# Channel-major tokens, a one-block start, and another entry to the second layer, in a two-layer hybrid backbone

## Chip, cores and metric

The kernel runs on one core of one Trainium2 chip. The metric is the device time of one execution in microseconds (us); less is better.

## The reference, cut to what matters

Two layers over 256 latent tokens `x` and 256 context tokens `ctx`, each 2048 wide, batch 1. Everything is float32.

```python
# layer 0                                   # layer 1
shift, scale, gate = adaln(c, ada_w[i], ada_b[i])      # silu(c) @ w + b, split in three
h = modulate(rms_norm(x, norm_g[i]), shift, scale)     # h*(1+scale)+shift
hc = the same for ctx with c_ctx                       # layer 0 alone
p = h @ w_in ; pc = hc @ w_in[:, COL_K:]    # p = h @ sc_in, four parts
neighbourhood attention (16 heads) on q, k, v, k_ctx, v_ctx
bidirectional SSD scan (32 heads)           # short gated convolution
out = concat(ya, yb) @ w_out                # out = (silu(g) * y) @ sc_out
x = x + gate * out                          # x = x + gate * out
```

The modulation vector of layer 0 needs `ada_w[0]`, 2048 x 6144 floats; of it, the scale columns (from 2048) and the shift columns (from 0) are needed before any projection can start, the gate only at the layer's end.

## The kernel before

One generator program records all instructions. Small tasks (generators) wait for a condition and an engine, and a planner (`Plan`) keeps a due time for each engine and tile: `pump` emits a task's next step when the planner's times say it is ready, `force` emits whatever is needed to go on. So the order of the instructions on each engine's queue is fixed when the program is built, out of costs written into `Plan`; among them `RATE`, the bytes per ns that it counts for a load, and 1500 ns that it adds to a transfer issued from another queue than SP's.

Large matmuls keep float32 accuracy by three products: an operand is split in a high part (a cast on ScalarE, `wH`, `hH`) and a low part (the difference, on VectorE, `wL`, `hL`), and high*high, low*high and high*low are summed. Weights come as pieces of 512 KB, 128 partitions x 1024 floats, into a pool of five `raw` buffers plus four borrowed ones (`PT`, `xtm`, `yi`), and are split into `NW` = 3 buffers `wH`/`wL`. All these loads stand in one queue, `loads`, and are issued by SP in that order (`issue`).

First stage of layer 0, over eight pairs `j` of 128-channel blocks `kb` = 2j, 2j+1:
- `x_load` brings tokens token-major, four tiles of 128 x 512 for each row tile of 128 tokens. `x_norm` squares each with a row sum on ScalarE or VectorE, takes the reciprocal root (`rstd`: VectorE, then a power on GpSimd) and scales the tile. `x_pair` turns it on TensorE (64 turns in all) into channel-major `xnT`. The context (`x_load(2)`, `x_load(3)`) is loaded behind the weights of pair 0.
- `ada_gen` multiplies the conditioning vectors (padded, `cpad`) by the modulation weights: for each pair, scale and shift, four pieces each of 512 rows x 256 columns. The sums go out of PSUM by ScalarE (L689), are turned, reduced and added on VectorE (L697 to L703) into `A0`, `S0`. Then `h = xnT*A0 + S0` is made once on ScalarE (high part, L719) and once on VectorE (L721), and subtracted (L725).
- The loop over `j` multiplies K, V (four row tiles, each into one bank, drained by `part_gen` into partial sums, L749 and L751), Q (two row tiles, accumulated over all pairs in two banks) and B (two banks). All matmuls are recorded at L188, turns at L192.

Behind it come the gate, dt, SSD and attention groups, all beside the large projections; then the output projection, columns 0 to 1023 first, then 1024 to 1535, then 1536 to 2047. `gemv_gen` multiplies the remaining modulation columns on VectorE (L776) in the background.

Entry to layer 1: `res_gen` forms `x1 = x + gate*out` for the last columns (L1506, L1509) and its squares (L1511); `turn_gen` turns `x1` to channel-major and scales it by `A1` into `late` (L1534); `norm_gen` waits for all four column groups, computes the norm factor, spreads it over the partitions through a diagonal and a matmul with ones (L1540 to L1544), and makes the sixteen blocks of `h1` (L1561, L1563, L1553).

Of the kernel before, what the change touches and what calls it, by code (L numbers as in the profile page):

```python
# [23 lines left out]
for _name, _w in (("c", 16), ("cc", 16), ("g0", 16), ("ab0", 48), ("g1", 16), ("ab1", 48), ("cw", 160), ("cb", 32),  # L24
                  ("sg", 16), ("qg", 1), ("kg", 1), ("scw", 48), ("dtb", 1), ("alog", 1), ("dcol", 16)):
    _off[_name] = (_n, _n + _w)
    _n += _w
NSMALL, NFIRST = _n, 96
# [3 lines left out]
for _name, _w in (("ident", 128), ("sel", 2), ("mhalf", 32), ("strip", 640), ("mask", 64)):  # L32
    _coff[_name] = (_n, _n + _w)
    _n += _w
NCONST, CFIRST = _n, 162


class Plan:
# [3 lines left out]
    RATE = 270.0  # L42
# [55 lines left out]
    def add(self, b):  # L98
# [10 lines left out]
        if op == "DMACopy":  # L109
# [4 lines left out]
            if e == "SP":  # L114
                self.dma = max(self.dma, s + 1000) + n / self.RATE
                done = free = self.dma + 1000
            else:
                done = free = max(self.dma, s + 1000) + n / self.RATE + 1500
# [23 lines left out]
def kernel(ctx: ExitStack, tc, x, cx, ada_w, ada_b, w_in, w_out, sc_in, sc_out, rpb, small, const,  # L142
# [96 lines left out]
    def may(task, hor, isurg):  # L239
# [5 lines left out]
        if nb and len(free_b) < nb + (0 if isurg else reserve[0]):  # L245
            return False
        now, t = plan.t["PE"], plan.t["ACT" if eng == "AQ" else eng]
# [17 lines left out]
    halfsplit = []  # L265
# [70 lines left out]
    E(DMA.dma_start(sm[:, :NFIRST], small[:, :NFIRST]))  # L336
    cs_ = st([128, NCONST], "const")
    E(DMA.dma_start(cs_[:, :CFIRST], const[:, :CFIRST]))
# [15 lines left out]
    def issue():  # L354

        while (loads or later) and (free_r or (loads and callable(loads[0]))):
# [12 lines left out]
            E(DMA.dma_start(v, w[r0:r0 + nb * 128, c0:c0 + n].rearrange("(b p) c -> p b c", p=128)))  # L369
            RAW[key] = (raw, v)  # L370

    nw = [0]
    room = [2]

    def weight(w, r0, nb, c0, n):
        loads.append(("w", nw[0], w, r0, nb, c0, n, room[0]))
        nw[0] += 1

    def split():
# [3 lines left out]
        if n == 64:  # L383

            W = WH[k % NW].rearrange("p (b c) -> p b c", b=nb)
# [9 lines left out]
        E(S.copy(H, v))  # L395
        E(V.tensor_tensor(out=Lo, in0=v, in1=H.bitcast(F32), op=ALU.subtract))  # L396
        HL[k] = (H, Lo)
        pos["split"] += 1
        give_raw(raw)
        issue()  # L400

    def split_half(b):

        raw, v = RAW[0]
        H, Lo = (w[0].rearrange("p (b c) -> p b c", b=2) for w in (WH, WL))
        E(S.copy(H[:, b], v[:, b]))

        def rest():
            E(V.tensor_tensor(out=Lo[:, b], in0=v[:, b], in1=H[:, b].bitcast(F32), op=ALU.subtract))  # L409
            if b:  # L410
                RAW.pop(0)
                HL[0] = (H, Lo)
                pos["split"] += 1
                give_raw(raw)
                issue()

        halfsplit.append(rest)

    def splits_try():
        if hold[0]:  # L420
            return
        while pos["split"] < pos["use"] + NW and pos["split"] in RAW:
            if plan.ready([RAW[pos["split"]][1]]) > max(plan.t["PE"], plan.t["ACT"]) + 300:
                return
            split()

    def use(ahead=0):
        k = pos["use"] + ahead
        while pos["split"] <= k:
# [4 lines left out]
            split()  # L434
        splits_try()
# [7 lines left out]
    def q_ada(j, *parts):  # L443
        for part, base in ((0, 2048), (1, 0)):
            if parts and part not in parts:
                continue
            for q in range(4):
                loads.append(("a", ("ada", j, part, q), ada_w[0], q * 512, 4, base + j * 256, 256, 2))
# [36 lines left out]
    q_ada(0)  # L485
    w_seg(0, CK, CV, CQ)
    loads.append(lambda: x_load(2))
    loads.append(lambda: x_load(3))
# [43 lines left out]
    ssq = st([128, 16], "ssq")  # L532

    def x_load(t):
        src = x if t < 2 else cx
        r0 = (t % 2) * 128
        for q in range(4):
            xt = st([128, 512], f"hH{4 * t + q}", name=f"xs{4 * t + q}")
            E(DMA.dma_start(xt, src[r0:r0 + 128, q * 512:(q + 1) * 512]))
            XS[4 * t + q] = xt  # L540

    x_load(0)
    x_load(1)
    issue()
    bs1 = st([128, 16], "bs1")
    E(V.tensor_scalar(out=bs1, in0=P_("ab0")[:, 16:32], scalar1=1.0, scalar2=None, op0=ALU.add))
    xnT = [st([128, 512], ("Bl", "Cl")[kb] if kb < 2 else f"hL{kb}", name=f"xm{kb}") for kb in range(KB)]
    rx = st([128, 4], "rx")

    def x_norm(t):  # L550
        yield when(lambda: 4 * t + 3 in XS and (t < 2 or ("h", 0, 0) in got))
        for q in range(4):
            xt = XS[4 * t + q]
            yield W_("ACT" if q % 2 == 0 else "DVE", xt)
            jk = tmp()
            if q % 2 == 0:
                E(S.activation(jk, xt, AF.Square, accum_out=ssq[:, 4 * t + q:4 * t + q + 1]))
            else:
                E(V.tensor_tensor_reduce(out=jk, in0=xt, in1=xt, scale=1.0, scalar=0.0, op0=ALU.mult, op1=ALU.add,
                                         accum_out=ssq[:, 4 * t + q:4 * t + q + 1]))  # L560
            give(free_t, jk)
        yield W_("DVE", ssq[:, 4 * t:4 * t + 4])
        E(V.tensor_reduce(out=rx[:, t:t + 1], in_=ssq[:, 4 * t:4 * t + 4], axis=AX.X, op=ALU.add))
        rstd(rx[:, t:t + 1], rx[:, t:t + 1], D, EPS, 1)
        for q in range(4):
            xt = XS[4 * t + q]
            yield W_("DVE" if q % 2 else "ACT", rx[:, t:t + 1])
            if q % 2 == 0:
                E(S.mul(xt, xt, rx[:, t:t + 1]))
            else:  # L570
                E(V.tensor_scalar(out=xt, in0=xt, scalar1=rx[:, t:t + 1], scalar2=None, op0=ALU.mult))

    def x_pair(k2, ts):

        yield W_("PE", *[XS[4 * t + k2 // 2] for t in ts], nb=1)
        ps = bank()
        n = 128 * len(ts)
        for k in range(2):
            kb = 2 * k2 + k
            for i, t in enumerate(ts):  # L580
                turn(ps[:, k * n + i * 128:k * n + (i + 1) * 128], XS[4 * t + kb // 4][:, (kb % 4) * 128:(kb % 4) * 128 + 128])
        yield W_("ACT", ps)
        o = slice(ts[0] * 128, ts[0] * 128 + n)
        E(S.copy(xnT[2 * k2][:, o], ps[:, 0:n]))
        E(V.tensor_copy(xnT[2 * k2 + 1][:, o], ps[:, n:2 * n]))
        give(free_b, ps)
        got.update(("xm", t, k2) for t in ts)

    def x_gen(c):

        ts = (2 * c, 2 * c + 1)
        for t in ts:
            yield from x_norm(t)
            if c:
                yield from x_pair(0, (t,))
        for k2 in range(c, KB // 2):
            yield from x_pair(k2, ts)
# [68 lines left out]

    def ada_gen():
        bc = lambda ap: ap.unsqueeze(2).to_broadcast([128, 2, 2])
        for j in range(8):
            k2 = slice(2 * j, 2 * j + 2)  # L670
            for part, dst in ((0, A0), (1, S0)):
                ps = None
                for q in range(4):
                    key = ("ada", j, part, q)
                    w_ = 2 if j == 0 else 4
                    if q % w_ == 0:
                        ks = [("ada", j, part, q + i) for i in range(w_)]
                        yield when(lambda: all(k in RAW for k in ks))
                        yield W_("PE", *[RAW[k][1] for k in ks], nb=0 if ps is not None else 1)
                    if ps is None:  # L680
                        ps = bank()
                    raw, v = RAW.pop(key)
                    for g in range(4):
                        mm(ps[32 * g:32 * g + 32, :256], cpad[:, 4 * q + g, :], v[:, g, :], q == 0, q == 3)
                    give_raw(raw)
                    issue()
                yield W_("ACT", ps)
                Rt = half()
                E(S.copy(Rt, ps[:, :256]))  # L689

                yield W_("PE", Rt)
                for b in range(2):
                    turn(ps[:, 256 + b * 128:384 + b * 128], Rt[:, b * 128:(b + 1) * 128])
                give(free_h, Rt)
                yield W_("DVE", ps)
                p2 = dst[:, k2, :]
                E(V.tensor_reduce(out=p2, in_=ps[:, 256:].rearrange("p (b g c) -> p b c g", b=2, c=32)[:, :, 0:2, :],  # L697
                                  axis=AX.X, op=ALU.add))
                if part == 0:
                    E(V.tensor_tensor(out=dst[:, k2, :], in0=p2, in1=bc(bs1[:, k2]), op=ALU.add))  # L700
                    E(V.tensor_tensor(out=dst[:, k2, :], in0=dst[:, k2, :], in1=bc(g0[:, k2]), op=ALU.mult))
                else:
                    E(V.tensor_tensor(out=dst[:, k2, :], in0=p2, in1=bc(P_("ab0")[:, k2]), op=ALU.add))  # L703
                give(free_b, ps)

# [832 lines left out]
    def norm_gen():  # L1538
# [19 lines left out]
        for kb in range(KB):  # L1558
# [5 lines left out]
            if kb:  # L1564
                low(kb - 1)
# [192 lines left out]
```

## Time and profile before

| | us |
|---|---|
| median of three runs | 1822.08 (1821.28 to 1822.44) |
| the profiled execution | 1820.64 |
| its span | 1818.9 |
| TensorE busy in the span | 1785.2 (98%) |
| VectorE busy | 1259.2 (69%) |
| ScalarE busy | 777.4 (43%) |
| moved by DMA | 376.9 MB, 207 GB/s in the mean |

A share of busy time is a mean over stages with different limits; what a change in one stage is worth is read from the gaps of the busiest engine there. L12 in a row is line 12 of the kernel before; PE is TensorE, PEld its weight loads, DVE VectorE, ACT ScalarE, POOL GpSimd, SP the load queue's engine.

### The profile page before, as it was taken

To read this page: it belongs to the slowest core of one execution; us is meant where nothing else is said; L and a number is where in the kernel's file an instruction comes from. 1 tells how busy PE (TensorE), PEld (TensorE's weight loads), DVE (VectorE), ACT (ScalarE), POOL (GpSimd) and SP (SyncE) were. 2 spreads that over 40 slices of the span, in tenths; PEclk is the share of its full clock that TensorE was granted. 3 is DMA by queue.
4 is the path that set the end of the run, shared out by engine and by line. 5 is a ranking of instruction groups with operands and counts; after the bars stand their busy time and mean duration, and the time that the engine had idled before them with its cause. 6 is when DMAs were issued, how large, how long until landed. Compare 5 with 4: busy or idle time off the path is not lost.

```text
span 1818.9 us, 26339 instructions
## 1 busy us (share of the span) xinstructions
PE 1785.2 (98%) x9959; PEld 1488.2 (82%) x9959; DVE 1259.2 (69%) x2039; ACT 777.4 (43%) x1369; POOL 28.5 (2%) x27
## 2 busy tenths in 40 slices
PE   6999999999999999999999999999999999999998
PEld 4677988888888888888887898788878888888877
DVE  5566785877575877565877677776567777776655
ACT  5323443445232454232444443654444444444442
POOL 0000100000000001000001000000000000000000
PEclk9999999999999999999999999999999999999999
DMA  9997644576565566545575557678676777777665
GB/s 330 334 299 256 203 132 131 167 223 178 169 185 191 154 199 182 192 139 177 163 225 162 169 146 246 206 226 289 220 243 209 222 251 228 231 248 221 186 203 156
DMA packets 249216, 376.90 MB, mean 207 GB/s; under 512 B 32656, under 2 KB 104048, under 8 KB 249088
## 3 DMA queue, kind: packets, MB, share of 16 engines
q1 hardware_dynamic: 239792, 366.64, 65.4%
q10 hardware_dynamic: 9296, 8.57, 1.4%
q8 instruction: 78, 1.28, 0.3%
q14 instruction: 50, 0.41, 0.1%
HBM read 368.70 MB, written 7.77 MB: 207 GB/s over the span
## 4 chain that ended last, share of the span: by engine, by line
PE 84%; issue 8%; DVE 2%; DMA 1%; ACT 1%; POOLq 0%; POOL 0%; SPq 0%; ACTq 0%; DVEq 0%
PE bank L188 82%; PE bank L192 2%; DVE wL L396 1%; DMA raw<-in_ada_w 1%; DMA tmp<-dram_csr 1%; ACT wH L395 0%; DVE tmp L1150 0%; DVE acc L776 0%; DVE h L1553 0%; DVE tmp L1331 0%; DVE hL L725 0%; DVE tmp L1691 0%; DVE tmp L721 0%; DVE tmp L1689 0%; DVE tmp L1334 0%
## 5 line engine op out<-in xcount | busy, mean ns | idle before, releaser
L395 ACT CAST wH<-raw 128x1024 fp32r<-128x1024 f32 (+1 forms) x439 | 458.4, 1046 | 730.4 <-PE bank L188 582.8
L396 DVE TENSOR_TENSOR wL<-raw,wH 128x1024 fp32r<-128x1024 f32 (+1 forms) x439 | 533.0, 1217 | 336.0 <-ACT wH L395 329.6
L188 PE MATMUL bank<-h,wH 128*128 128x512 f32 x1024 | 360.9, 398 | 2.0 <-DVE h L1553 2.0
L188 PE MATMUL bank<-hH,wH 128*128 128x256 f32 (+1 forms) x1040 | 353.4, 340 | 0.8 <-ACT wH L395 0.8
L188 PE MATMUL bank<-hL,wH 128*128 128x256 f32 (+1 forms) x1040 | 338.6, 326 | 0.0
L188 PE MATMUL bank<-hH,wL 128*128 128x256 f32 (+1 forms) x1024 | 331.7, 324 | 0.3 <-DVE wL L396 0.3
L188 PE MATMUL bank<-h,wL 128*128 128x256 f32 x1024 | 286.4, 280 | 0.4 <-DVE wL L396 0.4
L188 PE MATMUL bank<-wH,hH 128*128 128x512 f32 x640 | 257.9, 403 | 3.9 <-ACT hH L719 2.6
L188 PE MATMUL bank<-wL,hH 128*128 128x512 f32 x640 | 250.6, 392 | 0.0
L188 PE MATMUL bank<-wH,hL 128*128 128x512 f32 x640 | 249.7, 391 | 0.1
L188 PEld LDWEIGHTS bank<-h,wH 128*128 128x128 f32 x1024 | 193.0, 188 | 49.6 <-DVE h L1553 2.5
L776 DVE SCALAR_TENSOR_TENSOR acc<-raw,csil,acc 128x512 f32<-128x512 f32 x256 | 191.9, 750 | 42.7 <-DMA raw<-in_ada_w 37.7
L188 PEld LDWEIGHTS bank<-hH,wH 128*128 128x128 f32 x1040 | 196.8, 189 | 24.3 <-issue 7.4
L188 PEld LDWEIGHTS bank<-hL,wH 128*128 128x128 f32 x1040 | 197.1, 190 | 19.7 <-issue 4.8
L188 PEld LDWEIGHTS bank<-hH,wL 128*128 128x128 f32 x1024 | 194.2, 190 | 18.0 <-DVE wL L396 1.0
L188 PEld LDWEIGHTS bank<-h,wL 128*128 128x128 f32 x1024 | 193.5, 189 | 0.7 <-DVE wL L396 0.7
L188 PE MATMUL bank<-wH,mix 128*128 128x512 f32 x512 | 164.1, 396 | 0.3 <-ACT Vt L945 0.3
L188 PEld LDWEIGHTS bank<-wH,hH 128*128 128x128 f32 x640 | 120.2, 188 | 35.4 <-issue 6.2
L188 PEld LDWEIGHTS bank<-wH,hL 128*128 128x128 f32 x640 | 120.2, 188 | 26.3 <-DVE hL L725 0.6
L188 PEld LDWEIGHTS bank<-wL,hH 128*128 128x128 f32 x640 | 120.2, 188 | 24.7 <-DVE wL L409 0.5
L188 PEld LDWEIGHTS bank<-wH,mix 128*128 128x128 f32 x512 | 96.1, 188 | 22.3 <-issue 1.7
L188 PE MATMUL bank<-wL,mix 128*128 128x512 f32 x256 | 99.9, 390 | 0.0
(241 smaller groups left out, 1663.9 us busy)
## 6 DMA issues: line engine op xcount, KB each, us to landing
raw<-in_w_in SPq DMA_DIRECT2D x210, 512.0 KB
raw<-in_ada_w SPq DMA_DIRECT2D x162, 512.0 KB
raw<-in_sc_in SPq DMA_DIRECT2D x128, 512.0 KB
raw<-in_w_out SPq DMA_DIRECT2D x64, 512.0 KB
raw<-in_sc_out SPq DMA_DIRECT2D x32, 512.0 KB
tmp<-dram_csr SPq DMA_DIRECT2D x32, 256.0 KB
PT<-in_ada_w SPq DMA_DIRECT2D x14, 512.0 KB
xtm<-in_ada_w SPq DMA_DIRECT2D x9, 512.0 KB
```

What stands on the lines that cost most here:

```text
L188: E(T.matmul(o, l, r, start=start, stop=stop, skip_group_check=True))
L192: E(T.transpose(o, i, ident if k == 128 else ident[:k, :k]))
L395: E(S.copy(H, v))
L396: E(V.tensor_tensor(out=Lo, in0=v, in1=H.bitcast(F32), op=ALU.subtract))
L776: E(V.scalar_tensor_tensor(out=acc, in0=v[:, j], scalar=csil[:, 2 * k + j:2 * k + j + 1], in1=acc, op0=ALU.mult, op1=ALU.add))
```

## The change

1. **Tokens channel-major.** The host hands over `xT`, both token sets transposed, eight tiles of 128 channels x (2 blocks x 256 tokens) each. The turns, `xnT` and the scaled copies go. ScalarE squares each tile, VectorE adds its two blocks, TensorE sums over the channels with a column of ones.
2. **Norm factor spread by TensorE.** The factor of each token becomes a diagonal, and a matmul of ones with it puts it on all partitions (`Rx`). `h` is then `xT*A0*Rx` (VectorE), plus `S0` and rounded (ScalarE), and the low part from the same product (VectorE).
3. **Modulation weights of layer 0** come from an array `ada0` that the host has cut into contiguous pieces of 128 x 1024 floats.
4. **One block first.** Pair 0 is cut in two blocks: modulation for block 0 (four pieces), Q's weights, K and V of block 0 in one piece, then the same for block 1, then the context. The two small constant loads at the start go to ScalarE's queue (`DMA2`).
5. **Low halves apart.** A split now records the cast at once; the subtraction waits in `lows` and is recorded when the planner finds its cast done, or when a matmul needs it.
6. **New entry to layer 1.** The last three weight pieces of the output projection (`NTAIL` = 13) are multiplied for row tile 0 first, then for row tile 1; the sums of the first three column groups are added early and the norm factor is formed for each row tile by itself; eight of the turned blocks stay in PSUM and are scaled from there; 14 turns of the identity are put between (`keep_up`).
7. **Planner:** `RATE` 270 to 330, 1500 to 2500 ns for other queues' transfers. dt's decay matmuls are joined (14 calls to 8) and held back by 2500 ns of planned TensorE time.

```diff
-    RATE = 270.0
+    RATE = 330.0
...
-                done = free = max(self.dma, s + 1000) + n / self.RATE + 1500
+                done = free = max(self.dma, s + 1000) + n / self.RATE + 2500
...
-    E(DMA.dma_start(sm[:, :NFIRST], small[:, :NFIRST]))
+    E(DMA2.dma_start(sm[:, :NFIRST], small[:, :NFIRST]))
...
+            if kind == "a":
+                src = w[r0].rearrange("p (b c) -> p b c", b=nb)
+            elif kind == "kv":
+                src = w[r0:r0 + 128, COL_K:COL_X].rearrange("p (b c) -> p b c", b=2)[:, :, c0:c0 + n]
...
         E(S.copy(H, v))
+        lows.append((k, H, Lo, v, raw))
+        pos["split"] += 1
+
+    def low_part():
+        k, H, Lo, v, raw = lows.popleft()
         E(V.tensor_tensor(out=Lo, in0=v, in1=H.bitcast(F32), op=ALU.subtract))
         HL[k] = (H, Lo)
...
-    q_ada(0)
-    w_seg(0, CK, CV, CQ)
-    loads.append(lambda: x_load(2))
-    loads.append(lambda: x_load(3))
+    for u in range(2):
+        q_unit(u, 128)
+        if u == 0:
+            w_seg(0, CQ)
+        kv_seg(u)
+    loads.append(lambda: x_load(1))
...
+    def x_gen(c):
+        yield when(lambda: (c, 7) in XS)
+        r = rx[:, 2 * c:2 * c + 2]
+        ps = None
+        for k2 in range(KB // 2):
+            xt = XS[c, k2]
+            yield W_("ACT", xt)
+            jk = tmp()
+            E(S.activation(two(jk), xt, AF.Square))
+            yield W_("DVE", jk)
+            E(V.tensor_tensor(out=jk[:, :256], in0=jk[:, :256], in1=jk[:, 256:], op=ALU.add))
...
+            for t in range(2):
+                mm(ps[:, t:t + 1], jk[:, t * 128:(t + 1) * 128], one1[:, 0:1], k2 == 0 and t == 0, k2 == 7)
...
+        for t in range(2):
+            mm(ps[:, 128 + t * 128:256 + t * 128], one1, dg[:, t * 128:(t + 1) * 128], False, True)
...
+        E(S.copy(Rx[:, c * 256:(c + 1) * 256], ps[:, 128:384]))
...
+    def h_make(kb, cs):
+        yield when(lambda: all(("R", c) in got for c in cs))
...
+        for c in cs:
+            E(V.scalar_tensor_tensor(out=hf[:, o(c)], in0=xs[c], scalar=A0[:, kb, c:c + 1], in1=Rx[:, o(c)], op0=ALU.mult,
+                                     op1=ALU.mult))
+        yield W_("ACT", hf)
+        for c in cs:
+            E(S.activation(hH[kb][:, o(c)], hf[:, o(c)], AF.Identity, bias=S0[:, kb, c:c + 1], scale=1.0))
...
+        for c in cs:
+            E(V.scalar_tensor_tensor(out=hL[kb][:, o(c)], in0=hf[:, o(c)], scalar=S0[:, kb, c:c + 1],
+                                     in1=hH[kb][:, o(c)].bitcast(F32), op0=ALU.add, op1=ALU.subtract))
...
+    NTAIL = 13
...
-            hold[0] = len(passed) == 3 and ip == 15
+            hold[0] = len(passed) == 3 and ip >= NTAIL
+            if hold[0]:
+                if ip > NTAIL:
+                    continue
...
+                ws = [use(q) for q in range(16 - NTAIL)]
+                spawn(urgent, norm_gen(), 0, 1)
+                for t in range(2):
+                    for q, (H, Lo) in enumerate(ws):
+                        for b in range(2):
+                            i = 2 * order[NTAIL + q] + b
+                            mm_act([pss[0][t]], mH[i][:, 0, t * 128:(t + 1) * 128], mH[i][:, 1, t * 128:(t + 1) * 128],
+                                   H[:, b], Lo[:, b], False, NTAIL + q == 15 and b == 1)
+                        if t:
+                            used()
+                    got.add(("rows", 3, t))
+                    pump()
+                continue
...
+    def keep_up(n):
+        pt = bank()
+        for _ in range(n):
+            turn(pt[:, :128], ident)
+        give(free_b, pt)
...
     def norm_gen():
-        yield when(lambda: len(done) == 4)
-        E(V.tensor_reduce(out=r1, in_=ss1, axis=AX.X, op=ALU.add))
-        rstd(r1, r1, D, EPS, 2)
+        yield when(lambda: all(("sq", k, 1) in got for k in range(3)))
+        yield W_("DVE", ss1)
+        E(V.tensor_reduce(out=s3, in_=ss1[:, :, 0:3], axis=AX.X, op=ALU.add))
...
+        for t in range(2):
+            yield when(lambda: ("sq", 3, t) in got)
+            yield W_("DVE", ss1[:, t])
+            r = r1[:, t:t + 1]
+            E(V.tensor_scalar(out=r, in0=ss1[:, t, 3:4], scalar1=s3[:, t:t + 1], scalar2=1.0 / D, op0=ALU.add, op1=ALU.mult))
+            E(G.tensor_tensor(out=r, in0=r, in1=mhalf[:, :1], op=ALU.pow))
...
+            mm(rb[:, t * 128:(t + 1) * 128], ONES, dt_, t == 0, True)
+        keep_up(6)
```

464 lines of the change are left out of this document (262 added, 202 removed).

## The prediction

> **What bounds the kernel now.** I read the page's head first, then the busy time in six stretches that I cut where the work changes, then TensorE's timeline inside the stretches that have holes.
>
> ```profile
> span 1818.9 us, 26339 instructions
> ...
> L396 DVE TENSOR_TENSOR wL<-raw,wH 128x1024 fp32r<-128x1024 f32 (+1 forms) x439 | 533.0, 1217 | 336.0 <-ACT wH L395 329.6
> ```
>
> Busy time of the engines by stretch (length, then each engine's busy us, granted TensorE clock, DMA share, GB/s):
>
> ```profile
> 0.00:27.20 27.20, 10.91 (x100) 7.03 (x100) 11.01 (x36) 11.92 (x27) 1.33 (x6) 1.00 0.94 309
> 27.20:60.00 32.80, 29.13 (x206) 19.60 (x207) 22.30 (x58) 21.53 (x47) 1.60 (x4) 1.00 1.08 358
> 60.00:85.20 25.20, 23.93 (x175) 16.38 (x174) 12.83 (x24) 6.75 (x11) 0.00 (x0) 1.00 0.95 316
> 85.20:1353.50 1268.30, 1266.92 (x6999) 1057.20 (x6998) 889.60 (x1472) 525.10 (x987) 24.90 (x16) 1.00 0.65 197
> 1353.50:1364.00 10.50, 6.42 (x32) 5.12 (x31) 7.28 (x19) 7.62 (x19) 0.70 (x1) 0.84 0.26 93
> 1364.00:1384.00 20.00, 19.15 (x108) 16.13 (x107) 15.48 (x28) 11.82 (x18) 0.00 (x0) 1.00 0.49 152
> ```
>
> TensorE bounds it: from 85.2 to 1353.5 us it is idle for 1.4 us (1268.30 less 1266.92). The change leaves the large matmuls as they are, so it can win only holes: 16.3 us before 27.2, 3.7 us to 60, 1.3 us to 85.2, 4.1 us at the entry to layer 1, 0.9 us behind it. Inside these stretches (start, duration; the bracket is the idle time before, and what ended it):
>
> ```profile
> 13.79 1.08 PE L188 MATMUL bank<-raw,cpad 128*32 128x256 f32 x8 [13.79 <-DMA raw<-in_ada_w]
> ...
> 24.46 0.61 PE L188 MATMUL bank<-xtm,cpad 128*32 128x256 f32 x8
> 25.57 0.44 PE L192 MATMUL bank<-const,half 128*128 128x128 f32 x2 [0.49 <-ACT half L689]
> 27.23 0.50 PE L188 MATMUL bank<-wH,hH 128*128 128x512 f32 x1 [1.23 <-ACT hH L719]
> ...
> 37.78 0.50 PE L188 MATMUL bank<-wH,hH 128*128 128x512 f32 x1 [1.36 <-ACT hH L719]
> ...
> 50.44 0.48 PE L188 MATMUL bank<-wH,hH 128*128 128x512 f32 x1
> ...
> 60.02 0.39 PE L188 MATMUL bank<-wH,hH 128*128 128x512 f32 x1
> 62.53 0.40 PE L188 MATMUL bank<-wL,hH 128*128 128x512 f32 x1
> 62.86 1.93 PE L188 MATMUL bank<-raw,cpad 128*32 128x256 f32 x32
> 72.27 0.50 PE L188 MATMUL bank<-wH,hH 128*128 128x512 f32 x1 [1.16 <-DVE gt L751]
> 85.20 0.47 PE L188 MATMUL bank<-wH,hH 128*128 128x512 f32 x1
> ```
>
> 13.79 is the first modulation weight piece to land; 27.23 the first projection matmul. 37.78 and 50.44 open the two context row tiles of block pair 0, 60.02 pair 1, 85.20 pair 2. Prices: eleven steps from 60.02 to 62.53 make 0.228 us for each 512-column matmul; one part of a pair's modulation weights (x32) is 1.93 us.
>
> **First stage: the data.** How fast the pieces come depends on the length of the runs that a transfer reads. Rows of the DMA's rate by stretch (length, clock, share, GB/s), the first and third while 256-column modulation pieces flow (1 KB runs), the second while 512-column weights and tokens flow (2 KB runs):
>
> ```profile
> 16.00:18.00 2.00, 1.00 1.10 349
> 24.00:26.00 2.00, 1.00 1.06 389
> 42.00:44.00 2.00, 1.00 1.10 349
> ```
>
> The new modulation array has 4 KB runs. Going from 1 to 2 KB takes the time of a KB from 2.87 to 2.57 ns; half of that gain again gives 2.42 ns, an estimate of 412 GB/s. I take 400, with 349 (nothing gained) and 412 as ends.
>
> Before, 2.75 MB (two small constants, x at 2.10, one 0.52 MB piece) stood ahead of the landing at 13.79. The changed kernel sends the two constants over ScalarE's queue, so x starts two issues earlier on SP: about 0.9 us (their share of bytes stays). Its pieces then land, by my estimate, at 13.1, 14.4, 15.7 and 17.0 us (block 0), Q's weights 18.4, K/V of block 0 19.7, block 1's four pieces 21.1 to 25.0, K/V of block 1 26.4, the last context tile 31.8.
>
> Block 0's chain from its last piece: matmul, copy, turn, reduce, adds. Before, the same steps with one pass for h behind them took 2.8 us (24.46 to 27.23), so shift and scale stand 2 us behind the piece, at 19.0. Q's half split (ScalarE cast, VectorE low part) ends at 19.7, and one VectorE and one ScalarE pass later the first projection matmul starts at about 20.7 instead of 27.23. Little of these 6.5 us is kept: after six Q and twelve K/V matmuls (4.1 us) TensorE needs block 1, whose pieces are the same bytes as before. They land at 25.0, plus 2 us of the chain, plus the making of h: Q of block 1 starts at 28.5 to 31, and the 36 matmuls end at 33 to 36. Before they ended at about 35.8: 1.36 us of idle time and two turns ahead of 37.78. So the early start mostly fills a hole with the same work and opens a new one.
>
> Then the context. Its norm needs all eight tiles, landed by 31.8; ScalarE squares them in order behind block 1's h, so seven squares are still queued at 30 to 32.
>
> ```profile
> 5.02 0.63 ACT L557 ACTIVATE tmp<-xs 128x512 f32<-128x512 f32 x1 [2.18 <-DMA xs<-in_x]
> 22.35 0.37 ACT L689 COPY half<-bank 128x256 f32<-128x256 f32 x1 [0.66 <-PE bank L188]
> ```
>
> Seven at 0.63 end at 35 to 36.5; VectorE's add, the two 1-column matmuls, the power on GpSimd, two diagonals, the spreading matmuls (0.68 for the like pair, below) and the copy (0.37) add some 3 us, h another 1. The context rows start at 37 (squares in step with the landing) to 41; I take 39.5, later than 37.78. But then both context tiles are ready together, and the second doesn't wait until 50.44: the 64 turns of tokens are gone, and so is the work that stood between.
>
> From there the built order of the changed kernel has, up to the first K matmul of pair 2: 108 matmuls at 0.228 (24.6 us), six modulation parts at 1.93 (11.6 us; pairs 1 to 3, as before) and 12 turns (1.3 us, by an estimate of half a 512-column matmul each): 37.5 us. A hole of some 4 us stands ahead, so I add 1.7 us for a restart at half clock (below), and 1.2 us for one bank stall like that at 72.27. 39.5 + 37.5 + 2.9 = 79.9 against 85.2: **5.3 us won**, with ends 10.7 (37, no restart, no stall: 74.5) and 2 (41 and two more stalls: 83). Does data bind instead? Pair 3's last piece lands at about 72 at 400 GB/s and 78 at 349; 3 us of work stand behind it before pair 2: 75 or 81. At 349 it is level with the chain, so the run length is worth at most a microsecond here. Splitting the low parts off, and RATE at 330, only reorder VectorE's and the loads' work beside a busy TensorE: zero, with 1.4 us of idle time as all that could be won between 85.2 and 1353.5, and 2 us as a loss. The decay matmuls of dt fall from 14 calls to 8: under 1 us, taken as zero.
>
> **Entry to layer 1.** VectorE, ScalarE, GpSimd and TensorE in turn (last output-projection matmul; product and sum of x1; square; power; diagonals; spreading; scaling; low part; first layer 1 matmul; the first one past the slow pace, and the next pair):
>
> ```profile
> 1353.22 0.39 PE L188 MATMUL bank<-wH,mix 128*128 128x512 f32 x1
> ...
> 1354.48 0.68 DVE L1506 TENSOR_TENSOR tmp<-bank,tmp 128x512 f32<-128x512 f32 x1
> 1355.20 0.69 DVE L1509 TENSOR_TENSOR x1b<-tmp,tmp 128x512 f32<-128x512 f32 x1
> 1355.93 0.64 ACT L1511 ACTIVATE tmp<-x1b 128x512 f32<-128x512 f32 x1
> 1357.13 0.70 POOL L528 TENSOR_TENSOR r<-r,const 128x2 f32<-128x2 f32 x1 [143.48 <-DVE r L527]
> 1358.30 0.68 PE L188 MATMUL bank<-half,const 128*128 128x128 f32 x4 [1.37 <-DVE half L1544]
> 1359.02 0.75 DVE L1561 TENSOR_TENSOR PT<-PT,bank 128x256 f32<-128x256 f32 x2 [0.67 <-PE bank L188]
> 1360.02 0.48 DVE L1553 SCALAR_TENSOR_TENSOR h<-PT,M,h 128x256 fp32r<-128x256 f32 x1 [0.24 <-ACT h L1563]
> 1360.56 0.79 PE L188 MATMUL bank<-h,wH 128*128 128x512 f32 x1 [1.57 <-DVE h L1553]
> ...
> 1363.91 0.40 PE L188 MATMUL bank<-h,wH 128*128 128x512 f32 x1
> ...
> 1364.27 0.39 PE L188 MATMUL bank<-h,wH 128*128 128x512 f32 x1
> ```
>
> Before, 7.1 us lie between the end of the last issue (1353.45) and 1360.56. After, row tile 0 is finished 18 matmuls (4.1 us) ahead, and its sum, square and factor are done beside them. VectorE then has one low part (1.22) in hand until about 0.5 us after the end; product and sum of tile 1 end at 1.9, square and its read 2.8, power 3.6, diagonal and spreading 4.3, scaling, high and low part 5.8. So **1.3 us** less.
>
> The clock in the same place:
>
> ```profile
> 1360.00:1362.00 2.00, 1.44 (x4) 0.62 0.00 0
> 1362.00:1364.00 2.00, 2.00 (x8) 0.53 0.00 0
> ```
>
> After a stretch in which TensorE worked 2 us in 6, five pairs of matmuls took 3.35 us (1360.56 to 1363.91); at the pace behind them (0.36 a pair, 1363.91 to 1364.27) they take 1.8, so the slow clock cost 1.6 us. The 14 dummy turns and the eight real ones held back keep TensorE busy for about 4 of the 5.8 us. I count the 1.6 us as won; at the other end they are not won. The Trainium skill, "TensorE: Matmul & The Clock Gate", Part 1, says that the array falls to half rate after an idle window of about 3.4 us and needs about 3.4 us of steady work to return; the 3.35 us here agree.
>
> Against it: the tail holds all three weight buffers, so one piece of layer 1 is split ahead where two were. VectorE must then give, for 16 blocks, scaling (0.41 or 0.48), low part (0.48) and half a weight's low part (0.61): 1.5 us a block against 1.4 (four pairs at 0.36) on TensorE. It holds TensorE up 2 us, I estimate, against 0.9 now: 1.2 us lost. Together **1.7 us won**, from 3.5 won to 1 lost.
>
> Sum: 5.3 + 1.7 = 7.0. The profiled execution took 1820.64 (span 1818.9 and 1.7 around it), which makes 1813.6; the median of the runs, 1822.08, lies 1.4 above it, so I forecast 1815.0.
>
> **Rivals.**
> - *The context chain is in step with the data* (squares done by 32.5, rows at 37, no restart, no stall, no data wait): first stage 10.7 less 1 for data, entry 2.3, so 12 us won: 1810. For it: all eight tiles have landed by 31.8. Against: ScalarE takes its queue in order, and block 1's h stands ahead.
> - *Half clock at each new hole.* The new start has gaps of 4 us before 20.7, near 26 and near 38. If each costs 1.7 us and the later two delay what follows, with one more in pair 1, 3.4 us of the 5.3 go; if the dummy turns don't hold the clock, the entry loses 1.6: 7 - 5 = 2 won, 1820. For it: the row 0.53 after 2 busy us in 6. Against: in the old start, at 10.9 busy of 27.2 us, the clock row stays at 1.00. The skill's rule says that an idle window decides, so short bursts between the pieces could save it; it gives no price beyond the one above.
> - *Slower: the drain of K/V banks waits behind h on VectorE.* Now h takes eight two-input passes a pair (0.48, row of the low part: 3.84 us) where it took
>
> ```profile
> 106.05 0.73 DVE L721 TENSOR_SCALAR tmp<-xm,A,S 128x256 f32<-128x256 f32 x2
> 107.17 0.69 DVE L725 TENSOR_TENSOR hL<-tmp,hH 128x512 fp32r<-128x512 f32 x1 [0.39 <-ACT hH L719]
> ```
>
> 2.84. Three banks rotate, each filled by six matmuls (1.37 us). If the passes stand in front of two adds, TensorE stops as at 72.27, for 1.16 plus the added 1.0 us, in each of seven pairs: 15 us, 1815 + 15 = 1830. It decides once VectorE is held longer than three fills, 4.1 us. Against: VectorE is busy 12.83 of 25.2 us there.
> - *No change:* block 1 and the context set the pace, the chain starts at 41 with stalls, the entry is a draw: 1 to 2 us won, 1820.5.
>
> **How the numbers follow.** Forecast 0.50 (own range 1811.5 to 1818), in-step chain 0.20, half clock 0.13, slower 0.09, no change 0.08. The range 1808 to 1821 takes in all but the slower case and tails. A measurement tells this kernel from no change at about 0.2%, 3.6 us, so faster means below 1818.4: nearly all of the first two cases and a little of the others, 0.70; the same 0.21; slower 0.09.
>
> **What would show it.** In the changed profile: first projection matmul at 20 to 21.5; first context rows at 37 to 41; pair 2's first K matmul at 78 to 82; modulation pieces at 390 or more GB/s; last output matmul to first layer 1 matmul 5.5 to 6.2 us, and a clock of 1.00 behind it; VectorE ending TensorE's waits in the 20 us after. I am wrong if pair 2 starts at 84 or later, if the middle holds over 3 us of idle time, or if the entry is no shorter.

## The result, and the profile after

The changed kernel takes 1840.51 us in the median (1838.32 to 1845.98), the kernel before, run beside it, 1822.08: a ratio of 1.0101, 95% interval 1.0089 to 1.0114. It is 18.4 us slower where 7 us less were forecast. One of the five executions of the kernel before took 2536.68 us; it stands outside the ratio.

The heads of the two pages (span and instructions; TensorE's busy time, share and matmuls), first before, then after:

```profile
PE 1785.2 (98%) x9959; PEld 1488.2 (82%) x9959; DVE 1259.2 (69%) x2039; ACT 777.4 (43%) x1369; POOL 28.5 (2%) x27
```
```profile
span 1837.7 us, 26420 instructions
...
PE 1806.4 (98%) x10033; PEld 1495.1 (81%) x10033; DVE 1256.6 (68%) x2035; ACT 763.4 (42%) x1337; POOL 30.7 (2%) x26
```

TensorE's idle time did not grow: 1837.7 less 1806.4 is 31.3 us, against 33.7 before. It is busy 21 us longer. But that sum hides a shift. Ahead of 27.2 us the idle time fell from 16.3 to 8.7, because one-column sums (32 matmuls, 6.99 us from 5.59 on) now run while TensorE waits for data; behind it the idle time grew by some 5 us. The rest of the loss is time in which TensorE is busy: matmuls that take longer, or stand at half clock. After, in the stretches of the prediction (the last two joined):

```profile
0.00:27.20 27.20, 18.48 (x144) 14.73 (x145) 9.33 (x29) 10.06 (x18) 0.91 (x5) 1.00 0.96 361
27.20:60.00 32.80, 28.20 (x201) 20.07 (x200) 14.39 (x37) 12.55 (x25) 1.22 (x3) 0.84 0.76 286
60.00:85.20 25.20, 24.26 (x200) 15.92 (x198) 17.48 (x36) 8.30 (x16) 0.00 (x0) 1.00 0.95 347
85.20:1353.50 1268.30, 1260.57 (x6936) 1038.79 (x6933) 910.38 (x1520) 516.74 (x981) 27.46 (x16) 1.00 0.66 202
```

The early start filled the first stretch (18.48 us busy, was 10.91). The second has clock 0.84. The 1.00 of the first does not measure its start: the trace has no clock record before 26.06 us (none before 19.04 in the kernel before), and time without a record counts as full. The middle is idle for 7.7 us where it was 1.4.

Busy time hides where the loss arises, so I followed the large split-float matmuls, which stand in nearly the same order in all kernels here, numbered them in order of start, and took by how many us the one with the same number starts later than before. No. 36 opens the context rows, 72 pair 1, 144 pair 2; 576 ends the first stage, 4800 to 5400 runs into the output projection, 6000 stands in layer 1. Worked out from the traces, one execution of each kernel; the last three rows are kernels of experiments 1, 3 and 4:

```
matmul no.             0    36    72   144   576  4800  5400  6000  last
before, us          27.2  37.8  60.0  85.2 202.6  1103  1261  1400  1813
after               -5.5  +7.1  +0.5  +2.5  +5.7 +12.5 +18.9 +20.6 +18.9
moved 32 bytes      -5.7  +6.7  -0.1  +1.9  +3.7  +3.3  +8.3 +12.2 +11.6
 + constants late   -5.6  +6.8  -0.7  +1.3  +3.1  -1.0  +4.0  +1.0  +2.2
 + context's task   -6.2  +8.0  +1.3  -2.1  +1.4  -3.4  -1.5  -4.5  -4.6
```

Three places: the first stage, a steady loss of some 7 us over the middle, and some 8 us about the output projection.

TensorE's timeline after, first stage (first projection matmul; modulation matmuls at the slow and, behind 26.06 us, at the full pace; block 1's Q; then the one-column sums of the context's squares around block 1's V; the spreading; first context rows; pair 2), and the clock there:

```profile
21.76 1.22 PE L188 MATMUL bank<-wH,hH 128*128 128x512 f32 x2 [2.00 <-ACT hH L741]
...
24.61 1.08 PE L188 MATMUL bank<-PT,cpad 128*32 128x128 f32 x16
...
26.30 0.73 PE L188 MATMUL bank<-wH,hH 128*128 128x512 f32 x2
...
28.00 0.65 PE L188 MATMUL bank<-yi,cpad 128*32 128x128 f32 x16
...
32.24 0.72 PE L188 MATMUL bank<-wH,hH 128*128 128x512 f32 x2 [1.45 <-ACT hH L741]
...
35.63 2.73 PE L188 MATMUL bank<-QT,tmp 128*128 128x1 f32 x24
38.23 0.71 PE L188 MATMUL bank<-wH,hH 128*128 128x512 f32 x2
...
39.71 0.83 PE L188 MATMUL bank<-QT,tmp 128*128 128x1 f32 x4
42.16 1.22 PE L188 MATMUL bank<-half,QT 128*128 128x128 f32 x4 [1.62 <-DVE half L607]
44.90 0.79 PE L188 MATMUL bank<-wH,hH 128*128 128x512 f32 x1 [1.52 <-ACT hH L741]
...
87.71 0.39 PE L188 MATMUL bank<-wH,hH 128*128 128x512 f32 x1
```
```profile
38.00:40.00 2.00, 2.00 (x13) 1.74 (x12) 0.00 (x0) 0.32 (x1) 0.00 (x0) 0.93 1.05 412
40.00:42.00 2.00, 0.54 (x3) 0.45 (x3) 0.61 (x3) 1.27 (x3) 1.19 (x3) 0.50 0.27 107
42.00:44.00 2.00, 1.22 (x4) 0.92 (x4) 0.95 (x4) 0.37 (x1) 0.03 (x1) 0.50 0.08 15
```

So the early matmuls ran at the slow pace too. From 21.76 to 26.30 six projection and 32 modulation matmuls take 4.5 us; at the pace behind them (1.50 us for six, 1.01 for 32) they take 2.5. TensorE is never idle from 21.76 to 30.8 us, so these 2 us push block 1 back.

And about the end of the output projection: VectorE, then TensorE (a product of the background modulation columns, the low part behind it, and what TensorE waits for; then the last output matmul and the first of layer 1):

```profile
1367.74 1.54 DVE L816 SCALAR_TENSOR_TENSOR acc<-raw,csil,acc 128x512 f32<-128x512 f32 x2 [2.66 <-DMA raw<-in_ada_w]
1369.19 1.22 DVE L415 TENSOR_TENSOR wL<-raw,wH 128x1024 fp32r<-128x1024 f32 x1
```
```profile
1370.46 0.50 PE L188 MATMUL bank<-wL,mix 128*128 128x512 f32 x1 [1.90 <-DVE wL L415]
1370.80 0.95 PE L188 MATMUL bank<-wH,mix 128*128 128x512 f32 x2
...
1377.26 0.40 PE L188 MATMUL bank<-wH,mix 128*128 128x512 f32 x1
...
1383.18 0.50 PE L188 MATMUL bank<-h,wH 128*128 128x512 f32 x1 [0.92 <-DVE h L1650]
```

VectorE waits 2.66 us for a DMA; the low part that TensorE needs stands behind that product on VectorE's queue; TensorE stops, and then runs pairs at 0.95 us that take 0.63 at full clock.

### The profile page after: what moved, and what is told of

It reads as the page before. It is cut to its first block, busy times and chain, and to the rows that moved or that the text cites. A ratio compares the mean times of both kernels' runs of the same rounds, so it can differ in the third digit from the quotient of the medians.

```text
span 1837.7 us, 26420 instructions
## 1 busy us (share of the span) xinstructions
PE 1806.4 (98%) x10033; PEld 1495.1 (81%) x10033; DVE 1256.6 (68%) x2035; ACT 763.4 (42%) x1337; POOL 30.7 (2%) x26
## 5 line engine op out<-in xcount | busy, mean ns | idle before, releaser
L408 ACT CAST wH<-raw 128x1024 fp32r<-128x1024 f32 x437 | 456.1, 1044 | 718.2 <-PE bank L188 570.6
L415 DVE TENSOR_TENSOR wL<-raw,wH 128x1024 fp32r<-128x1024 f32 x437 | 530.1, 1216 | 261.1 <-ACT wH L408 259.2
L188 PEld LDWEIGHTS bank<-hH,wL 128*128 128x128 f32 x1024 | 192.7, 188 | 18.4 <-DVE wL L415 0.8
L188 PE MATMUL bank<-wH,mix 128*128 128x512 f32 x512 | 167.8, 404 | 2.3 <-ACT Vt L1003 2.3
L188 PEld LDWEIGHTS bank<-wH,hH 128*128 128x128 f32 x640 | 120.1, 189 | 40.5 <-issue 9.2
```

The costliest lines, as they stand in the source:

```text
L188: E(T.matmul(o, l, r, start=start, stop=stop, skip_group_check=True))
```

## Experiments

Times are medians beside the kernel before on the same chip; "+" is against that median.

**1. Place of the activations, low halves, planner.** In both kernels the weights' buffers lie at the same addresses, but the activations behind the constants do not: the wider constants, and another order of the buffers, moved them. An unused tile of 8 columns moves them by 32 bytes more:

```diff
     cs_ = st([128, NCONST], "const")
+    st([128, 8], "shift")
```

> The kernel before with one unused tile of 8 columns (32 bytes) placed behind the constants, so every later buffer (activations, h, small tables) starts 32 bytes further on, as in the changed kernel; no instruction changes. Theory A (place in memory): in the changed kernel the activations' buffers start at odd multiples of 32 bytes where before they started at multiples of 64, and that makes each 512-column matmul 3 to 6 ns longer; with about 3500 of them in layer 0 the shift alone should cost 10 to 18 us: 1832 to 1840, with the 512-column pace going from 0.227-0.229 to about 0.233 us. Theory B (low halves apart load the memory or the engines beside the matmuls): no change, 1822. Theory C (order of work by the planner's new constants): no change, 1822.

> The changed kernel with the same unused tile of 8 columns, which puts the activations' buffers back on multiples of 64 bytes; no instruction changes. Theory A: 10 to 18 us faster than the changed kernel: 1823 to 1831. Theories B and C: no change, 1840.

The kernel before, moved: 1827.47, +7.0 (ratio 1.0042, 1.0030 to 1.0055). The changed one, moved: 1832.76, +12.3 (1.0070, 1.0057 to 1.0084), some 6 to 8 us less than without. So where the buffers lie is worth about 7 us in both, less than the 10 to 18 that were expected; the rest of the loss is something else.

```diff
         lows.append((k, H, Lo, v, raw))
         pos["split"] += 1
+        low_part()
```

> The changed kernel with the low part of every full weight piece made right behind its high part again, as before. Theory B: most of the 18 us comes back, 1824 to 1830, with the 512-column pace back at 0.227-0.229. Theory A: the pace stays at 0.233 and the time at 1836 to 1843. Theory C: likewise 1836 to 1843.

1854.95, +34.4: the opposite of theory B. Low halves apart help this kernel by 14 us; joined, the first stage loses 6 us more (No. 576 at +12.0) and the entry 11 more (No. 5400 at +24.9, No. 6000 at +37.6), where TensorE then waits 6.5 us in seven places for ScalarE's h.

```diff
-    RATE = 330.0
+    RATE = 270.0
...
-                done = free = max(self.dma, s + 1000) + n / self.RATE + 2500
+                done = free = max(self.dma, s + 1000) + n / self.RATE + 1500
```

> The changed kernel with the planner's old DMA rate (270) and landing delay (1500). Theory C: the order of the middle comes back, its waits on Vt and wL (2.3, 1.2 and 1.9 us) shrink, 5 to 10 us faster, 1830 to 1835. Theories A and B: within 3 us of 1840, pace still 0.233.

1837.97, +17.5: only 2.5 us less. But the curve has two halves: No. 576 at +11.3 (was +5.7), the last at +14.4 (was +18.9; the traced execution is the fastest of four). The old constants win some 10 us behind the first stage and lose 5.6 in it. I had expected one sign.

**2. Who stands in front of the low parts?**

```diff
+                while lows and not first_[0]:
+                    low_part()
                 raw, v = RAW.pop(("gem", n, k))
```

> The changed kernel with the 8-column tile that puts the activations back on multiples of 64 bytes, and with every low part whose high part has been issued made before VectorE takes the next piece of the modulation vector's weights (the product that waits for a DMA). Theory D (of what remains after the shift, most is that low parts stand on VectorE behind a product that waits for its DMA, so TensorE stops for wL and restarts at half clock): the waits of 1.4, 2.4 and 3.6 us on wL at 1170, 1249 and 1361 us of the shifted run go, with the slow 2 to 3 us behind the last: 6 to 10 us faster than 1832.8, so 1823 to 1827. Theory E (the remaining loss is more instructions or a worse order elsewhere): 1830 to 1834.

1833.14, +12.2: no gain; theory D as I put it fell. The rows show why, VectorE and TensorE in this kernel:

```profile
1361.01 1.54 DVE L819 SCALAR_TENSOR_TENSOR acc<-raw,csil,acc 128x512 f32<-128x512 f32 x2 [5.96 <-DMA raw<-in_ada_w]
1362.47 1.22 DVE L416 TENSOR_TENSOR wL<-raw,wH 128x1024 fp32r<-128x1024 f32 x1
```
```profile
1363.74 0.80 PE L188 MATMUL bank<-wL,mix 128*128 128x512 f32 x1 [5.28 <-DVE wL L416]
```

VectorE reaches the product at 1355.05 us; ScalarE starts the cast that the low part needs at 1355.51. So no low part was there to be put ahead when the product was recorded. What is wrong is the time at which the planner places the product: VectorE reaches it 6 us before its piece lands.

In the kernel before, the new constants alone:

> The kernel before with the planner's DMA rate at 330 and the landing delay of ScalarE's queue at 2500, nothing else. Theory D: VectorE waits longer for DMA (the kernel before has 39 us of such waits behind 85 us, the changed one 78), but low parts are made right behind the high ones there, so little reaches TensorE: 1820 to 1824. If the planner's constants alone cost time, 1826 to 1832.

1833.64, +12.7 (1.0072, 1.0057 to 1.0087): the expectation of theory D was wrong, the constants alone cost time here too. But not all of it in the way of the changed kernel: the first projection matmul starts 4.9 us later (32.17 instead of 27.23), because 32 turns of tokens, which stood between two modulation pieces (at 16.21), now stand in one row behind them (at 25.66). No. 576 is at +5.7, No. 4800 at +6.8, No. 5400 at +11.8, the last at +11.3: some 6 us arise behind the first stage.

VectorE's waits for these pieces (us in all, times, longest) in the kernel before, after, in this one, and in experiment 3:

```profile
DVE acc L776 <- DMA raw<-in_ada_w: 37.7, 33, 3.8
```
```profile
DVE acc L816 <- DMA raw<-in_ada_w: 67.3, 48, 4.7
```
```profile
DVE acc L776 <- DMA raw<-in_ada_w: 62.3, 50, 3.4
```
```profile
DVE acc L818 <- DMA raw<-in_ada_w: 40.3, 35, 2.4
```

**3. The new constants for the start alone.** In `Plan.add`, with the 8-column tile:

```diff
+            rate, lag = (330.0, 2500) if self.t["PE"] < 200e3 else (270.0, 1500)
```

> The changed kernel with the 8-column tile, and with the planner's new constants (330, 2500) used only for the first 200 us of its own clock, the old ones (270, 1500) behind that. Theory F (the new constants let the planner believe that pieces land sooner than they do; VectorE and ScalarE then stand in front of a DMA, and the low parts queued behind them stop TensorE in the output projection): the loss between 1103 and 1401 us (8.8 us in the shifted run) shrinks to 2 to 4, VectorE's waits for DMA fall from 88 to about 50 us, and the time to 1823 to 1827. If the constants matter only by chance of order: 1830 to 1835.

1819.92, -1.3 (0.9997, 0.9988 to 1.0006): better than expected. Place and constants explain the whole loss against the kernel before: 12.3 us became none. VectorE's waits are back at 40.3 us, TensorE's idle time behind No. 576 falls from 12.1 to 5.1 us (6.9 in the kernel before), and No. 4800 to 6000 lose 2.0 us instead of 8.9. `RATE` and the delay were not tried apart.

**4. The start.** The context's h gets a task of its own, and the planner's rate is 400 for 60 us, 330 to 200 us, then 270:

```diff
-        for kb in range(2):
-            yield from h_make(kb, (1,))
         for j in range(1, 8):
             yield from ada_unit(2 * j, 256)
+            yield when(lambda: ("h", 1, 1) in got)
...
+    def hc_gen():
+        yield when(lambda: ("h", 1, 0) in got)
+        for kb in range(2):
+            yield from h_make(kb, (1,))
```

> As the kernel before it in this list, with two more edits to the start: the context's h for block pair 0 is made by a task of its own, so that the modulation matmuls of pair 1 needn't stand behind it, and the planner's rate is 400 in the first 60 us (the traces show 380 to 420). Theory G (the start lost because the context's chain leaves TensorE idle for 3 us and more and at half clock behind that, with pair 1's modulation matmuls ready): pair 2 starts 3 to 5 us sooner than in the run without these edits, and the time is 3 to 5 us less. If the start is bound by data or by VectorE instead: no change.

1816.04, -5.2 (0.9977, 0.9966 to 0.9987): as theory G has it, 3.9 us less than experiment 3, and faster than both kernels. Its timeline and clock (L190 is the matmul line here): pair 1's modulation matmuls fill the hole, the clock stays at 1.00 there, pair 2 opens at 83.12 instead of 87.71 (86.5 in experiment 3). The context rows themselves come no sooner. The task and the rate of 400 were changed together, so what each is worth stays open.

```profile
39.48 0.71 PE L190 MATMUL bank<-half,QT 128*128 128x128 f32 x4
40.12 0.64 PE L190 MATMUL bank<-raw,cpad 128*32 128x256 f32 x8
...
45.75 0.51 PE L190 MATMUL bank<-wH,hH 128*128 128x512 f32 x1
...
83.12 0.39 PE L190 MATMUL bank<-wH,hH 128*128 128x512 f32 x1
...
1351.71 0.39 PE L190 MATMUL bank<-wH,mix 128*128 128x512 f32 x1
...
1357.92 0.50 PE L190 MATMUL bank<-h,wH 128*128 128x512 f32 x1 [0.92 <-DVE h L1658]
```
```profile
42.00:44.00 2.00, 1.51 (x26) 0.88 (x26) 0.50 (x4) 0.65 (x2) 0.00 (x0) 1.00 0.93 281
```

**5. What is it about the place?** All in the kernel before, instructions unchanged, with the unused tile put elsewhere or made wider. Where a buffer lies is read from the built programs.

> The kernel before with the weights' buffers (wH, wL) alone 32 bytes further on; all else in its place. If it is the stationary operand that has to start on a multiple of 64 bytes: layer 0, where h is stationary, keeps its pace, layer 1, where the weights are stationary to h, gets slower: 1822 to 1828. If any of the two operands off the multiple costs the same 3 to 5 ns: 1826 to 1832 (as the shift of the activations). If it is the two operands' position against each other that counts, as with the activations shifted: the same changes, 1827.

1829.04, +8.1. 

> The kernel before with both the weights' buffers and the activations 32 bytes further on. If the two operands' position against each other counts: they agree again, 1820 to 1822. If each operand off the multiple of 64 costs for itself: 1830 to 1836. If only the stationary one counts: 1827 to 1833.

1830.04, +9.1. These two edits do not do quite what was meant. A second unused tile stands behind the weights' buffers, so all that follows moves by it as well: in the first kernel the weights lie 32 bytes further on and h 64, in the second 32 and 96. So h lies 32 bytes further from the weights in the first, as in experiment 1, and 64 in the second, as in the kernel moved by 64 below. The matmuls take what they take there: first moved by 32 and the first of these, then the second (the one moved by 64 follows further down):

```profile
L188 PE MATMUL bank<-wH,hL 128*128 128x512 f32 x640 | 252.0, 394 | 0.1
...
L188 PE MATMUL bank<-wL,mix 128*128 128x512 f32 x256 | 101.2, 395 | 0.0
```
```profile
L190 PE MATMUL bank<-wH,hL 128*128 128x512 f32 x640 | 252.1, 394 | 0.1
...
L190 PE MATMUL bank<-wL,mix 128*128 128x512 f32 x256 | 101.2, 395 | 0.0
```
```profile
L190 PE MATMUL bank<-wH,hL 128*128 128x512 f32 x640 | 253.1, 396 | 0.1
...
L190 PE MATMUL bank<-wL,mix 128*128 128x512 f32 x256 | 100.8, 394 | 0.0
```

From start to start, high weights by low h take 234.8 and 234.9 ns at 32 bytes more, 236.3 and 236.7 at 64, and 230.9 in the kernel before. In the first of the two kernels h lies where it lies in the one moved by 64, and its pace is that of 32. So in these kernels the distance between the two operands sets the pace, and not the place of one.

> The kernel before with layer 1's h (the moving operand of its input projection) 32 bytes off the multiples of 64 while layer 0's h stays on them (the slots are 8 columns wider and h takes the first or the last 512). If the place of the two operands against each other sets the pace as in the two shifted runs (layer 1's 512-column matmul 4.5 and 5.7 ns shorter there): 4 to 6 us faster than before, 1815 to 1817. If the shifts cost by something else: 1820 or more.

1825.22, +4.0: a miss. The shorter layer 1 matmuls that I had seen in moved kernels are no handle. The wider slots also spread the sixteen low buffers over eight places, 64 bytes apart, in each layer.

> The kernel before with the unused tile at 16 columns, so that the activations move by 64 bytes instead of 32. If only the place within 64 bytes counts: no change, 1820 to 1822. If any move of the buffers costs: 1825 to 1829, as at 32 bytes.

1828.85, +7.6: multiples of 64 bytes are not it. Then perhaps no place at all, but any new build?

> The kernel before with one comment line more: every instruction and every address as before. If the place of the buffers costs the 7 to 9 us in the moved kernels: 1820 to 1822, no change. If any new build of the program differs by that much: 1826 to 1830.

1820.69, -0.1 (0.9998, 0.9989 to 1.0007). 

> The changed kernel with one comment line more, nothing else. Place: 1839 to 1842. Any new build: anything between 1830 and 1842.

1841.07, +20.3. A new build changes nothing.

> The kernel before with the unused tile at 128 columns: the activations move by 512 bytes. If the place counts with a period of 512 bytes or a divisor above 64: 1820 to 1822. If not: 1826 to 1830, as for 32 and 64 bytes.

1821.40, +0.6 (1.0000, 0.9991 to 1.0009). 

> The kernel before with the unused tile at 32 columns: the activations move by 128 bytes. Period of 128 bytes: 1820 to 1822, no change. Period of 256 or 512: 1826 to 1830.

1830.58, +9.3 (1.0049, 1.0035 to 1.0063). So it is the place: 32, 64 and 128 bytes cost 7 to 9 us, 512 cost nothing. If the cost repeats, its period is 256 or 512 bytes; 256 was not tried. The groups by form show it in the mean ns of one (here the high weights by low h, and the low weights in the output projection): before, moved by 64, by 128, by 512, then after (whose second line holds some matmuls at half clock):

```profile
L188 PE MATMUL bank<-wH,hL 128*128 128x512 f32 x640 | 249.7, 391 | 0.1
...
L188 PE MATMUL bank<-wL,mix 128*128 128x512 f32 x256 | 99.9, 390 | 0.0
```
```profile
L188 PE MATMUL bank<-wH,hL 128*128 128x512 f32 x640 | 252.9, 396 | 0.1
...
L188 PE MATMUL bank<-wL,mix 128*128 128x512 f32 x256 | 100.9, 394 | 0.0
```
```profile
L188 PE MATMUL bank<-wH,hL 128*128 128x512 f32 x640 | 251.8, 394 | 0.1
...
L188 PE MATMUL bank<-wL,mix 128*128 128x512 f32 x256 | 101.1, 395 | 0.0
```
```profile
L188 PE MATMUL bank<-wH,hL 128*128 128x512 f32 x640 | 250.3, 392 | 0.1
...
L188 PE MATMUL bank<-wL,mix 128*128 128x512 f32 x256 | 100.0, 391 | 0.0
```
```profile
L188 PE MATMUL bank<-wH,hL 128*128 128x512 f32 x640 | 252.1, 396 | 0.9 <-DVE hL L746 0.9
...
L188 PE MATMUL bank<-wL,mix 128*128 128x512 f32 x256 | 102.0, 398 | 3.7 <-DVE wL L415 3.7
```

Three to five ns on some 3000 matmuls of this kind (weights moving, h, mix or y stationary) make 9 to 15 us, an estimate; that is the size of the 7 to 9 us, or somewhat more. In layer 1, where h moves, the 512-column matmuls get shorter by up to 6 ns and the 256-column ones longer by 3 to 4, 1024 of each, so little is left of that. In the kernel before, 24 of h's 32 buffers lie at the same offset from a multiple of 512 bytes as the weights; in the changed one 25 lie 96 bytes short of it, and with the tile 64. Why the distance counts stays open.

**6. Place in the best version.** Without the tile, and with 24 columns instead of 8, which puts 25 of h's 32 buffers where most of them lay before (128 beyond a multiple of 512, as the weights):

> The kernel with the planner's constants by stretch (400, 330, 270) and the context's h in a task of its own, without the 8-column tile, so with the activations where the changed kernel has them. If the place is worth the same in another order: 7 to 9 us slower than with the tile, 1823 to 1825. If the gain of the move was of another kind: 1816.

1825.20, +4.4: 9 us slower than with the tile, about as expected. 

> The version with the planner's constants by stretch and the context's h in a task of its own, with an unused tile of 24 columns instead of 8: 25 of the 32 buffers of h start on multiples of 128 bytes (with 8 columns 7 do, the others at 64, with none nearly all at 32). If the distance from the multiples of 128 sets the price: faster than 1816.0 by 3 to 7 us, 1809 to 1813. If 64 off is as good as 0 in this order: 1816. If it is another trait: anything up to 1825.

1813.68, -7.6 (0.9959, 0.9947 to 0.9972): the fastest here, 2.4 us less than with 8 columns, a little under the expected 3. The two intervals overlap, so this last step is not clear of the noise.

## Why the prediction was wrong, point by point

- **"Splitting the low parts off, and RATE at 330, only reorder ... zero", with 2 us as the worst loss.** This step failed most. Behind the first 200 us the constants cost some 13.5 us in the changed kernel (from +12.3 to -1.3); in the kernel before they cost 12.7, of which some 5 arise before the first projection matmul. I read from the 1.4 us of idle time that the middle had nothing to win and took that for nothing to lose. An engine that is idle for 1.4 us in 1268 has no slack for the waits that a new order brings: here it is idle for 7.7. The low parts apart were worth 14 us to this kernel, not zero.
- **Missing: the place of the buffers, 6 to 8 us.** Neither the sum nor a rival had it, nor could the instruction order show it. The diff shows the wider constants; that the buffers behind them move was not followed up.
- **First stage, 5.3 us won.** The steps up to the first projection matmul nearly held (20.7 forecast, 20 to 21.5 as the sign, 21.76 measured), the pieces came at 382 to 420 GB/s (400 taken), and the squares ended where I put them (35.8). What I left out there is the half clock until 26.06: it cost 2 us, and block 1's Q opened at 32.24 instead of 28.5 to 31. The step that failed most is what I counted behind the squares: "the two 1-column matmuls" are 32 instructions of 0.11 us for the context, 3.6 us on TensorE, partly behind block 1's V; and the chain from there took 4.4 us (40.5 to 44.90) where I had 4 from the squares on. Rows at 44.90 instead of 39.5, and pair 2 at 87.71 instead of 79.9. Experiment 4 turns 1.3 us lost there (experiment 3) into 2.1 won by filling the hole, so the hole and the clock were the loss, not the data. The far end of this term was added wrongly as well: 41, 37.5, 2.9 and two stalls of 1.2 make 83.8, so 1.4 us won and not 2.
- **Entry, 1.7 us won.** The mechanism held. From the start of the last output matmul to the first of layer 1 are 5.9 us after and 6.2 in experiment 4; 6.0 were forecast (5.8 from the end of that issue), and 7.3 it was before, and the clock there stays at 1.00. From No. 5400 to 6000, experiments 3 and 4 win 3.0 us each. In the changed kernel the wait for the tail's low part and its half clock, both gone with the old constants in experiment 3, turn that into 1.7 lost.
- **Rivals.** Half clock happened, at the first projection matmuls, from 39.7 to about 50 us and behind the tail's wait, but is a part of the loss only. My argument against it misread a row: the 1.00 of the old start holds no record before 19.04 us, and my own lines show eight modulation matmuls at 1.08 us (13.79) and at 0.61 (24.46). The slower rival, K and V banks drained late, did not: no such wait is among TensorE's longer ones. The loss came from a mechanism that I had not listed. My own signs caught it: pair 2 behind 84, and 7.7 us idle in the middle.
- **Not tried.** The contiguous modulation pieces, dt's joined decay matmuls and the turns that hold the clock at the entry were not taken out one by one.

## What to carry to other kernels

When the bound engine is 98% busy, ask of every edit that only reorders what it can cost, not what it can win; here a planner's two constants cost some 13 us in either kernel. Follow a wait to the head of the queue: TensorE waited for a low part, VectorE for a DMA that the planner had believed landed. When a tile changes its size, compare the addresses of everything behind it, and time an unchanged kernel with its buffers moved before blaming the edit; an unused tile, too, moves all that stands behind it. And check a clock of 1.00 against the duration of equal matmuls.

## What the runs showed of the hardware that I had not expected

- A move of the activations by 32, 64 or 128 bytes within their partitions, away from the weights' buffers, costs 7.0, 7.6 and 9.3 us of 1821, by 512 bytes none (0.6, within the interval). With the weights moved as well, the distance between the two decides (experiment 5). The Trainium skill, "SBUF — State Buffer", Operand start alignment, asks only for a multiple of the element size and says that it is about legality, not speed; these runs show that the place has a price in speed.
- The clock fell to 0.50 at 39.71 us although TensorE's longest idle time in the 9 us ahead was 1.45 us. The Trainium skill, "TensorE: Matmul & The Clock Gate", Part 1, speaks of an idle window of about 3.4 us; no such window is in the trace ahead of the fall. TensorE had run 2.73 us of one-column matmuls in a row, but such a row alone does not decide it: in experiment 3's kernel 2.74 us of them stand in a row at 36.18 and the clock stays at 1.00 until 44.48, while with the old constants (experiment 1) it falls at 41.52 behind 1.84 us in a row, 0.95 us more and 1.14 us of idle time. In experiment 4, with at most 1.84 us in a row and TensorE busy behind them, it stays at 1.00. The changes of the clock lie multiples of 3.41 us apart (26.06, 39.71, 49.95 after; 27.41, 44.48, 47.89 in experiment 3), so where a row falls between them may count as well. None of this was tried by itself.
